# Hybrid HGRN and chunk-MLP backbone on one core: layer 1's modulation computed in two output phases instead of the HGRN stage

## The chip, the cores and the metric

The kernel runs on one core of a Trainium2 chip. The metric is device time in microseconds (us) of one execution; smaller is better. Engines: PE (TensorE) multiplies matrices into PSUM, PEld is its weight load, DVE (VectorE) and ACT (ScalarE) work elementwise, POOL (GpSimd) does small odds and ends, SP (SyncE) issues all the large DMA loads from one queue. Three runs of the kernel before took 2491.83, 2493.34 and 2493.70 us: the median is 2493.34 us. The execution that the profiler recorded took 2490.62 us, with a span of 2488.9 us from first to last instruction.

## The reference

Two layers over a 512-token latent stream `x` of width 1024 and, in layer 0, a 256-token context. Each layer is a half-step SwiGLU, a token mixer (layer 0: bidirectional HGRN2 with 8 heads; layer 1: a chunked spatial-gating MLP), and another half-step SwiGLU. Every sub-layer is modulated by vectors that come from the conditioning vector `c`:

```
def modulation(cond, w_mod, b_mod):
    m = jax.nn.silu(cond) @ w_mod + b_mod          # 9 vectors of 1024 per layer
def modulate(x, m, k):
    return x * (1 + m[..., 3*k+1, :]) + m[..., 3*k, :]
def post_norm_update(x, y, m, k, g, b):
    return layer_norm(DN_ALPHA * x + m[..., 3*k+2, :] * y, g, b)
```

So a layer needs nine modulation vectors, called channels here: 0, 1 and 2 (shift, scale, gate) for the first half-FFN, 3 to 5 for the mixer, 6 to 8 for the second half-FFN. Each is the product of one 1024-vector with a 1024 x 1024 matrix of its own (4 MB).

## The kernel before

Nearly all matrix products are done with float32 operands split into a high and a low part (`split`, L134: ACT copies the high part, DVE subtracts for the low one) and three matmuls per product (`mm3`, L146). A 128 x 1024 block of weights is loaded into one of three `raw` buffers and split into one of six `w` buffers (`unit`, L139).

The stages follow each other: layer 0's first half-FFN for latent and context, the HGRN mixer, layer 0's second half-FFN, layer 1's first half-FFN, the chunk MLP, layer 1's second half-FFN. A half-FFN has an input phase (`FeedIn` or `FeedSums`) and an output phase (`OutPhase`). `FeedSums.rest` (L577) goes over the hidden blocks f; a block loads its gate weights into `raw` and its up weights into `rawu` (two buffers) and forms sums of them in a tile `e` (two buffers); these three belong to the pool `sp`. In a block PE accumulates several products into one bank `psc`, and ACT copies that bank out (`kept`, L621) before PE adds the next product to it. `OutPhase.run` (L370) goes twice (half `hf` of the output columns) over 11 weight units; a unit needs one `w` split and two splits `hs` of the hidden blocks, and 24 matmuls. After the last unit come normalisation, transposes and the next stage's operand, which needs the channels of the next sub-layer (`operand_cols`, L226).

A modulation channel is a Python generator (`mod_task`, L172) of eight steps: a step loads 512 KB of the matrix (`mraw`, two buffers) and lets DVE multiply it with the row of silu(c) and sum, in two halves (`mod_dot`, L164, into a throwaway tile `junk` with the sums in `acc`; each half is a SCALAR_TENSOR_TENSOR and a DVE_READ_ACCUMULATOR). After the eighth step a few small instructions finish the channel; gates also need a PE transpose and a store. `mod_step(n)` (L203) adds n steps of credit and issues what the credit allows, behind a given instruction; `made(key)` (L216) issues whatever is still missing. The row of silu(c) comes from `silu_row` (L157): a load that broadcasts 4 KB to all 128 partitions and one ACT activation.

Instructions are written in program order with these hints; a scheduler then sets the order on each engine, and each engine runs its list in that order. DMA loads wait in SP's list for the buffer that they write.

In the HGRN stage (L912 to L1220) a loop of nine rounds runs over eight heads: round h projects head h (`proj_forget`, `proj_silu`) while the scores, states, outputs and gating of the heads before are worked off. `on` (L1149) is DVE's normalised output of a head, `pto` (L1155) its PE transpose, `Sc` (L1119) the scaled states that the output matmuls `po` (L1137 to L1139) read, `pkc` (L1094) the first matmul of a head's states. Four channels of layer 1 (1, 0, 4, 3) are queued in round 0 (L1197) and worked off at seven steps a round (L1205); `late_outputs` (L918) closes their pool in round 6 and opens the space for the last four heads' outputs. The remaining channels 5, 7, 6, 8 of layer 1 are computed in the chunk MLP (L1294, two steps per block, L1338).

Of the kernel before, what the change touches and what calls it, by code (L numbers as in the profile page):

```python
# [10 lines left out]
F32 = mybir.dt.float32  # L11
F32R = mybir.dt.float32r
# [6 lines left out]
P = 128  # L19
D = 1024  # L20
# [50 lines left out]
def backbone_kernel(  # L71
# [100 lines left out]
    def mod_task(modp, srow, l, ch, conds):  # L172
        accs = {c: modp.tile([P, KD, 2], F32, tag=f"acc_{c}", name=f"acc_{c}", bufs=2) for c in conds}
        for f in range(KD):
            raw = modp.tile([P, D], F32, tag="mraw", name="mraw", bufs=2)
            nc.sync.dma_start(raw, mod_w[l, ch, f])
            for c in conds:
                mod_dot(modp, accs[c][:, f, :], raw, srow[c])
            yield
        for c in conds:  # L180
            key = (l, ch, c)
            dot = modp.tile([P, KD], F32, tag="dot", name="dot", bufs=2)
            nc.vector.reduce_sum(dot, accs[c], axis=AX.X)
            if ch % 3 == 2:
                nc.vector.tensor_tensor(dot, dot, mbT[:, l, ch, :], ALU.add)
                pg = bank("pg")
                nc.tensor.transpose(pg[:KD, :P], dot, ident)
                row = modp.tile([KD, P], F32, tag="mrow", name="mrow", bufs=1)
                nc.vector.tensor_copy(row, pg[:KD, :P])
                gate_row[key] = dram.tile([1, D], F32, name=f"gr_{l}_{ch}_{c}")  # L190
                nc.sync.dma_start(gate_row[key].rearrange("o (f p) -> (o f) p", p=P), row)
            else:
                mod_col[key] = const.tile([P, KD], F32, name=f"mc_{l}_{ch}_{c}")
                nc.vector.scalar_tensor_tensor(
                    mod_col[key], dot, float(ch % 3), mbT[:, l, ch, :], ALU.add, ALU.add
                )

    def queue_mod(modp, srow, l, ch, conds):
        mod_queue.append(mod_task(modp, srow, l, ch, conds))
# [711 lines left out]

    with sbuf(name="hgo", bufs=1) as hgo, ExitStack() as late:  # L912
        hts = [hgo.tile([P, 2, T], F32R, name=f"ht{h}") for h in range(NH - NLATE)]
        early = ExitStack()
        modp = early.enter_context(sbuf(name="modp1", bufs=1, side="right"))
        srow = {"x": silu_row(modp, "x")}

        def late_outputs():  # L918
            for ch in (1, 0, 4, 3):
                made((1, ch, "x"))  # L920
            early.close()
            hgo2 = late.enter_context(sbuf(name="hgo2", bufs=1, side="right"))
            hts.extend(hgo2.tile([P, 2, T], F32R, name=f"ht{h}") for h in range(NH - NLATE, NH))

        with sbuf(name="hg", bufs=1) as hg:
            mask = []
# [237 lines left out]
            )  # L1164
            prev, done, last = None, None, None
            for h in range(NH + 1):
                if h == NH - NLATE + 2:
                    late_outputs()
                if h < NH:
                    n0, last = proj_forget(h, 0)  # L1170
                else:
                    op.lead(0, 1)
                if done and (h < NH or 0 == 0):
                    with tc.issue_after(last.ins):
                        gated(*done)
                if prev:
                    r0, r1 = prev
                    kTc = transposed([r.kk[:, NT + s, :] for r in prev for s in range(NTC)])
                    kT0 = transposed([r0.kk[:, s, :] for s in lat_order(0)[:-1]])
                    near_scores(r0)  # L1180
                    far_scores(0, r0)
                if h == NH and 0 == 1:
                    gated(*done)
                if h < NH:
                    n1, _ = proj_forget(h, 1)
                if prev:
                    context_states(h - 1, prev, kTc)
                    kT1 = transposed([r1.kk[:, s, :] for s in lat_order(1)[:-1]])
                    latent_states(h - 1, 0, r0, kT0)
                    far_scores(1, r1)  # L1190
                    latent_states(h - 1, 1, r1, kT1)
                if h < NH:
                    q, _ = proj_silu(h, 0, "q")
                    for r in (n0, n1):
                        ready = queries(r, q)
                    if h == 0:
                        for ch in (1, 0, 4, 3):  # L1197
                            queue_mod(modp, srow, 1, ch, ["x"])
                        first = ready
                else:  # L1200
                    if 0 == 2:
                        gated(*done)
                    op.lead(0, 2)
                if h < NH:
                    mod_step(7, first)  # L1205
                if prev:
                    on = outputs(h - 1, prev)
                    g, last = proj_silu(h - 1, 3, "g")
                    done = (h - 1, on, g)
                if h < NH:  # L1210
                    prev = (n0, n1)
# [11 lines left out]
    with sbuf(name="sp2", bufs=1) as sp, sbuf(name="hp2", bufs=1) as hp, bpools() as bp:  # L1223
        hget = f2.rest(hp, sp)
        xm = new_xm(xmp, "xm", T)
        f3 = FeedSums(
            1, 0, xm, NT,
            lambda i: hp.tile([P, T], F32, tag="h", name="h", bufs=NF).rearrange("p (k t) -> p k t", k=2),
        )
        op = OutPhase(  # L1230
            hget, NF, ffn_units(0, 1), NT, 0, 2, "x", 0.5, lambda t: x2[t], True, (1, 0),
            xm, lambda t: x3[t], f3, tail=3,
        )
        op.nhs, op.affine = 8, (0, 1)
        op.run(bp)
        hget = f3.rest(hp, sp)
        xm = new_xm(xmp, "xm", T)

        gin = GateIn(xm, lambda i: hp.tile([P, T], F32, tag="h", name="h", bufs=NF).rearrange("p (k t) -> p k t", k=2))
        op = OutPhase(  # L1240
            hget, NF, ffn_units(1, 0), NT, 1, 0, "x", 0.5, lambda t: x3[t], True, (1, 1),
            xm, lambda t: x4[t], gin, tail=3,
        )
        op.nhs, op.affine = 8, (0, 2)
        op.run(bp)


    with ExitStack() as vhp_stack:
# [9 lines left out]
        with sbuf(name="cm", bufs=1) as cm, ExitStack() as late:  # L1258
# [32 lines left out]
                stat.append((mv[:, 0:1], rstd))  # L1291
            modp = early.enter_context(swap("modp3"))
            srow = {"x": silu_row(modp, "x")}
            for ch in (5, 7, 6, 8):  # L1294
                queue_mod(modp, srow, 1, ch, ["x"])
            cu = late.enter_context(sbuf(name="cu", bufs=1))

# [5 lines left out]
            for gi in range(NG):  # L1303
                vt = vs[gi]
                for t in range(NT):
                    mean, rstd = stat[t]
                    nc.vector.tensor_scalar(vt[:, t, :], vt[:, t, :], mean, rstd, ALU.subtract, ALU.mult)
                ht = vhp.tile([P, 3, T], F32, tag="vh", name="ht")
                if gi == NG - 1:
                    for ch in (5, 7, 6, 8):  # L1310
                        made((1, ch, "x"))
                    early.close()
                for ci in range(3):
                    w = unit(cm_wu[gi * 3 + ci])
                    psu = bank("pscu")
                    feat_mm(psu, w, xm, 0, T)
                    u = cu.tile([P, T], F32, tag="u", name="u", bufs=2)
                    nc.scalar.activation(u, psu, AF.Gelu_apprx_tanh)
                    if gi == NG - 1 and ci == 2:
                        op.lead(0, 2)  # L1320
                    pss = bank("pscs")
                    for t in range(NT):
                        nc.tensor.matmul(
                            pss[:, t * P : (t + 1) * P], vt[:, t, ci * P : (ci + 1) * P], wsT[:, gi, :],
                            start=True, stop=True,
                        )

                    j = gi * 3 + ci
                    add = cu.tile([P, 1, P], F32, tag="add", name="add", bufs=2)
                    nc.vector.scalar_tensor_tensor(  # L1330
                        add[:, 0, :], wsum[:, gi, :], gb[:, 1, j : j + 1], bsr[:, gi, :], ALU.mult, ALU.add
                    )
                    tb = cu.tile([P, NT, P], F32, tag="tb", name="tb", bufs=2)
                    nc.vector.scalar_tensor_tensor(
                        tb, pss.rearrange("p (n t) -> p n t", t=P), gb[:, 0, j : j + 1],
                        add.broadcast_to([P, NT, P]), ALU.mult, ALU.add,
                    )
                    mod_step(2)  # L1338
                    nc.vector.tensor_tensor(ht[:, ci, :], tb.rearrange("p n t -> p (n t)"), u, ALU.mult)
                hs.append(ht)  # L1340
# [91 lines left out]
```

## Time and profile before

| | before |
|---|---|
| three runs, median (lowest to highest) | 2493.34 us (2491.83 to 2493.70) |
| profiled execution: time, span | 2490.62 us, 2488.9 us |
| PE, PEld busy | 2430.3 us (98%), 2185.5 us (88%) |
| DVE, ACT busy | 1919.8 us (77%), 1133.7 us (46%) |
| mean DMA traffic | 147 GB/s |

A page of the profile gives busy time per engine, a picture of the span in 40 slices, the chain of waits that ends last, and groups of instructions with the idle time of their engine ahead of them. Windows count busy time of every engine in a stretch; a timeline lists instructions by start. A matmul's end is modelled and matmuls overlap, so PE's busy share says little about small gaps; how far apart the same instruction of two rounds starts says more.

### The profile page before, as it was taken

What the parts mean: (1) busy time and instruction counts of PE and PEld (TensorE: products, weight loads), DVE (VectorE), ACT (ScalarE), POOL (GpSimd) and SP (SyncE); (2) the same over time, 40 slices, a digit from 0 to 9 for tenths busy, and PEclk for the clock granted to TensorE, in tenths of its full rate; (3) what the DMA queues carried; (4) which work ended last, traced back from release to release, by engine and by line L of the source; (5) the groups of instructions that cost most, each with busy time, mean ns of one, the idle gap of its engine ahead of it and who ended that gap; (6) DMA issues with size and microseconds to landing.
All of it is one profiled execution on the core that took longest, in us unless ns stands there. A gap on an engine that the chain in (4) does not pass through costs nothing.

```text
span 2488.9 us, 37370 instructions
## 1 busy us (share of the span) xinstructions
PE 2430.3 (98%) x14619; PEld 2185.5 (88%) x14619; DVE 1919.8 (77%) x3426; ACT 1133.7 (46%) x1725; POOL 46.5 (2%) x83
## 2 busy tenths in 40 slices
PE   7999999999988999999999999999999999999998
PEld 5888889988877888899988999988988888999986
DVE  7965678685699986998765988757889665998765
ACT  4222434453444543555643555534552233555641
POOL 0000000000000000000000000000000000000001
PEclk9999999999999999999999999999999999999999
DMA  8855556874345223333334333333347343332332
GB/s 319 299 196 199 177 183 198 286 257 140 102 137 160 77 60 117 133 132 107 119 103 134 103 110 111 111 95 123 119 160 260 129 148 106 140 128 102 102 110 73
DMA packets 106706, 364.92 MB, mean 147 GB/s; under 512 B 12392, under 2 KB 13600, under 8 KB 106528
## 3 DMA queue, kind: packets, MB, share of 16 engines
q1 hardware_dynamic: 106528, 362.53, 43.9%
q8 instruction: 114, 1.87, 0.3%
q14 instruction: 64, 0.52, 0.1%
HBM read 349.87 MB, written 12.61 MB: 146 GB/s over the span
## 4 chain that ended last, share of the span: by engine, by line
PE 80%; DVE 13%; DMA 2%; ACT 2%; issue 1%; POOL 1%; SPq 0%; POOLq 0%; DVEq 0%; ACTq 0%
PE y L150 8%; PE y L148 8%; PE y L149 8%; PE psf L149 5%; PE psf L150 5%; PE psf L148 5%; PE psc L148 5%; PE psc L150 5%; PE psc L149 5%; PE pse L148 2%; PE pse L150 2%; PE pse L149 2%; PE pscu L148 2%; PE pscu L149 2%; PE pscu L150 2%; DVE junk L170 1%
## 5 line engine op out<-in xcount | busy, mean ns | idle before, releaser
L136 DVE TENSOR_TENSOR w<-raw,w 128x1024 fp32r<-128x1024 f32 (+2 forms) x446 | 505.9, 1138 | 153.9 <-ACT w L135 153.0
L135 ACT ACTIVATE w<-raw 128x1024 fp32r<-128x1024 f32 (+2 forms) x446 | 439.5, 987 | 332.1 <-PE y L150 89.0
L150 PE MATMUL y<-w,hs 128*128 128x512 f32 x984 | 383.1, 389 | 1.0 <-DVE hs L136 1.0
L148 PE MATMUL y<-w,hs 128*128 128x512 f32 x984 | 383.3, 389 | 0.0
L149 PE MATMUL y<-w,hs 128*128 128x512 f32 x984 | 382.9, 389 | 0.0
L136 DVE TENSOR_TENSOR hs<-h,hs 128x512 fp32r<-128x512 f32 (+1 forms) x220 | 136.4, 637 | 143.6 <-ACT hs L135 143.4
L135 ACT ACTIVATE hs<-h 128x512 fp32r<-128x512 f32 (+1 forms) x220 | 127.3, 588 | 251.7 <-PE y L150 241.7
L150 PEld LDWEIGHTS y<-w,hs 128*128 128x128 f32 x984 | 184.7, 188 | 40.4 <-DVE hs L136 1.9
L148 PEld LDWEIGHTS y<-w,hs 128*128 128x128 f32 x984 | 184.7, 188 | 38.6 <-ACT hs L135 0.2
L149 PEld LDWEIGHTS y<-w,hs 128*128 128x128 f32 x984 | 184.7, 188 | 38.0
L148 PE MATMUL psf<-xm,w 128*128 128x512 f32 (+1 forms) x544 | 192.8, 361 | 17.8 <-ACT xm L135 17.1
L149 PE MATMUL psf<-xm,w 128*128 128x512 f32 (+1 forms) x544 | 194.4, 358 | 0.7 <-DVE xm L136 0.5
L150 PE MATMUL psf<-xm,w 128*128 128x512 f32 (+1 forms) x544 | 193.9, 357 | 0.8 <-DVE w L136 0.8
L170 DVE SCALAR_TENSOR_TENSOR junk<-mraw,srow_x 128x512 bf16<-128x512 f32 x256 | 167.3, 688 | 8.9 <-DMA mraw<-in_mod_w 8.8
L148 PE MATMUL pse<-f,w 128*128 128x256 f32 x480 | 136.1, 284 | 3.7 <-ACT w L135 3.7
L148 PE MATMUL psc<-f,w 128*128 128x256 f32 x480 | 136.1, 284 | 0.0
L150 PE MATMUL pse<-f,w 128*128 128x256 f32 x480 | 135.9, 283 | 0.0
L148 PE MATMUL psc<-xm,w 128*128 128x256 f32 x480 | 135.8, 283 | 0.0
L149 PE MATMUL psc<-xm,w 128*128 128x256 f32 x480 | 135.8, 283 | 0.0
L149 PE MATMUL pse<-f,w 128*128 128x256 f32 x480 | 135.8, 283 | 0.0
L150 PE MATMUL psc<-xm,w 128*128 128x256 f32 x480 | 135.8, 283 | 0.0
L149 PE MATMUL psc<-f,w 128*128 128x256 f32 x480 | 135.8, 283 | 0.0
(305 smaller groups left out, 5987.1 us busy)
## 6 DMA issues: line engine op xcount, KB each, us to landing
raw<-in_ffn_w_in SPq DMA_DIRECT2D x160, 512.0 KB, 4.3
mraw<-in_mod_w SPq DMA_DIRECT2D x144, 512.0 KB, 4.3
raw<-in_ffn_w_out SPq DMA_DIRECT2D x110, 512.0 KB, 3.6
rawu<-in_ffn_w_in SPq DMA_DIRECT2D x60, 512.0 KB, 3.5
x<-x SPq DMA_DIRECT2D x36, 512.0 KB, 3.4
raw<-in_hg_wf SPq DMA_DIRECT2D x32, 512.0 KB, 3.8
raw<-in_cm_wu SPq DMA_DIRECT2D x24, 512.0 KB, 4.6
raw<-in_cm_w_out SPq DMA_DIRECT2D x24, 512.0 KB, 3.5
```

What stands on the lines that cost most here:

```text
L135: nc.scalar.activation(dst_hi, src, AF.Copy)
L136: latest[0] = nc.vector.tensor_tensor(dst_lo, src, dst_hi.bitcast(F32), ALU.subtract)
L148: nc.tensor.matmul(ps, ah, bh, start=start, stop=False, **kw)
L149: nc.tensor.matmul(ps, ah, bl, start=False, stop=False, **kw)
L150: return nc.tensor.matmul(ps, al, bh, start=False, stop=stop, **kw)
L170: nc.vector.scalar_tensor_tensor(junk, w[:, c], 1.0, s[:, c], ALU.mult, ALU.mult, dst[:, i : i + 1])
```

## The change

Channels 1, 0, 4 and 3 of layer 1 leave the HGRN stage, with their pool, their row of silu(c) and `late_outputs`; the space for the last four heads' outputs is now taken at the stage's start. Channel 5 leaves the chunk MLP. Channels 1 and 0 are queued for the output phase of layer 0's second half-FFN at one step per weight unit, and channels 4, 3 and 5 for the output phase of layer 1's first half-FFN at one and a half. They use idle tiles of the input phases: the matrix loads go to the two `rawu` buffers, the row of silu(c) to one `e` buffer, and all small tiles (`acc`, `junk`, `dot`, `mrow`) are cut from the other `e` buffer. The throwaway `junk` is now float32 and one buffer instead of bfloat16 and two.

```diff
+    class Scraps:
+        def __init__(self, pool, small, ring):
+            self.pool, self.ring, self.at, self.got = pool, ring, 0, {}
+            self.small = pool.tile([P, D], F32, tag=small, name=small, bufs=2)
+        def tile(self, shape, dtype, tag, name, bufs=1):
+            if tag == "mraw":
+                return self.pool.tile(shape, dtype, tag=self.ring, name=self.ring, bufs=2)
...
+            t = self.small[: shape[0], a : a + int(np.prod(shape[1:]))]
...
+    def scraps(sp, l, chs):
+        s = sp.tile([P, D], F32, tag="e", name="e", bufs=2)
+        nc.sync.dma_start(s, cond[CI_OF["x"]].partition_broadcast(P))
+        nc.scalar.activation(s, s, AF.Silu)
+        small = Scraps(sp, "e", "rawu")
+        for ch in chs:
+            queue_mod(small, {"x": s}, l, ch, ["x"])
...
-        early = ExitStack()
-        modp = early.enter_context(sbuf(name="modp1", bufs=1, side="right"))
-        srow = {"x": silu_row(modp, "x")}
-        def late_outputs():
...
+        hgo2 = late.enter_context(swap("hgo2"))
+        hts.extend(hgo2.tile([P, 2, T], F32R, name=f"ht{h}") for h in range(NH - NLATE, NH))
...
-                if h == NH - NLATE + 2:
-                    late_outputs()
...
-                    if h == 0:
-                        for ch in (1, 0, 4, 3):
-                            queue_mod(modp, srow, 1, ch, ["x"])
-                        first = ready
...
-                if h < NH:
-                    mod_step(7, first)
...
         op.nhs, op.affine = 8, (0, 1)
-        op.run(bp)
+        scraps(sp, 1, (1, 0))
+        op.run(bp, None, 1)
...
         op.nhs, op.affine = 8, (0, 2)
-        op.run(bp)
+        scraps(sp, 1, (4, 3, 5))
+        op.run(bp, None, 1.5)
...
-            for ch in (5, 7, 6, 8):
+            for ch in (7, 6, 8):
                 queue_mod(modp, srow, 1, ch, ["x"])
```

DVE in the HGRN stage, from the sum `ssum` of a head's scores to the gated output `ht`. `junk,acc_x<-mraw,srow_x` is half a modulation step. Before:

```order
L1133 TENSOR_TENSOR ssum<-sT_5512,sT_5513 128x512
L988 TENSOR_TENSOR g<-psq,g 128x512
L1018 TENSOR_SCALAR X<-psfl 128x512
L170 SCALAR_TENSOR_TENSOR junk,acc_x<-mraw,srow_x 128x512 x2
L136 TENSOR_TENSOR w<-raw,w 128x1024
L170 SCALAR_TENSOR_TENSOR junk,acc_x<-mraw,srow_x 128x512 x2
L1144 TENSOR_REDUCE ss<-on 128x4
L1019 TENSOR_SCALAR X<-psfc 128x256
L1145 TENSOR_SCALAR ss<-ss 128x4
L136 TENSOR_TENSOR w<-raw,w 128x1024
L170 SCALAR_TENSOR_TENSOR junk,acc_x<-mraw,srow_x 128x512 x2
L1149 TENSOR_TENSOR on_6390<-po,rs 128x512
```

Six halves stand between the two splits and the reduction that lead to `on`; with the change no such row is left in this stage.

ACT near the end of layer 0's second input phase. `e<-e` is the activation silu(c) in the `e` buffer; `sc<-psc` are the copies of the bank that PE goes on accumulating into. With the change:

```order
L651 ACTIVATE sc<-psc 128x256
L135 ACTIVATE w<-rawu 128x1024
L135 ACTIVATE w<-raw 128x512
L222 ACTIVATE e<-e 128x1024
L651 ACTIVATE sc<-psc 128x256
L667 ACTIVATE silu<-silu 128x256
L135 ACTIVATE w<-raw 128x1024
L670 ACTIVATE silu<-psc 128x256
L135 ACTIVATE w<-e 128x1024
```

Before, the same list has no `e<-e` row: `sc<-psc` follows `w<-raw 128x512` at once. One `w<-e` comes after it and then none, so the activation stands two blocks ahead of the phase's end. The second input phase has the same picture.

SP at the same place, with the change (`raw<-in_ffn_w_out` are the output phase's weight units, `rawu<-in_mod_w` the modulation's loads, `e<-in_cond` the row of c):

```order
L628 DMA raw<-in_ffn_w_in 128x1024
L630 DMA rawu<-in_ffn_w_in 128x1024
L141 DMA raw<-in_ffn_w_out 128x1024
L221 DMA e<-in_cond 128x1024
L176 DMA rawu<-in_mod_w 128x1024
L141 DMA raw<-in_ffn_w_out 128x1024
L176 DMA rawu<-in_mod_w 128x1024
L141 DMA raw<-in_ffn_w_out 128x1024 x5
L176 DMA rawu<-in_mod_w 128x1024 x3
L141 DMA raw<-in_ffn_w_out 128x1024
```

Before, loads of the next input phase's `rawu` stand where the first two modulation loads stand now, and the weight units follow without anything between them.

## Rows read from the trace of the kernel before

**Rows 1.** The page: span, busy time, the chain of waits by engine, and the group of the output phases' matmuls that has any idle time of PE ahead of it (busy us, mean ns, idle us).

```profile
span 2488.9 us, 37370 instructions
...
PE 2430.3 (98%) x14619; PEld 2185.5 (88%) x14619; DVE 1919.8 (77%) x3426; ACT 1133.7 (46%) x1725; POOL 46.5 (2%) x83
...
PE 80%; DVE 13%; DMA 2%; ACT 2%; issue 1%; POOL 1%; SPq 0%; POOLq 0%; DVEq 0%; ACTq 0%
...
L150 PE MATMUL y<-w,hs 128*128 128x512 f32 x984 | 383.1, 389 | 1.0 <-DVE hs L136 1.0
```

**Rows 2.** Busy time of all engines in six windows of the HGRN stage, each from one head's first `pkc` to the next head's (stretch, its length, then PE, PEld, DVE, ACT, POOL busy with their instruction counts, granted clock, DMA share, GB/s).

```profile
681.10:729.40 48.30, 40.06 (x229) 35.14 (x228) 46.02 (x127) 21.61 (x33) 1.92 (x1) 0.93 0.44 141
729.40:773.10 43.70, 38.91 (x228) 34.33 (x227) 42.24 (x112) 19.41 (x29) 1.02 (x1) 0.96 0.46 146
773.10:813.20 40.10, 37.32 (x229) 32.90 (x228) 38.10 (x97) 19.08 (x29) 1.31 (x1) 1.00 0.46 143
813.20:852.20 39.00, 37.33 (x229) 32.90 (x228) 36.41 (x89) 18.62 (x29) 1.01 (x1) 1.00 0.29 95
852.20:889.60 37.40, 37.02 (x227) 32.77 (x227) 31.34 (x72) 18.71 (x31) 1.01 (x1) 1.00 0.20 57
889.60:927.00 37.40, 37.04 (x228) 32.77 (x227) 31.33 (x72) 18.68 (x30) 1.01 (x1) 1.00 0.19 57
```

**Rows 3.** The modulation's DVE work alone (tile `junk`) in the first four of these windows.

```profile
681.10:729.40 48.30, 14.07 (x43) 0.93 0.44 141
729.40:773.10 43.70, 12.17 (x38) 0.96 0.46 146
773.10:813.20 40.10, 8.02 (x23) 1.00 0.46 143
813.20:852.20 39.00, 2.86 (x10) 1.00 0.29 95
```

**Rows 4.** Who PE waited for: first from 641 to 852 us, then (last row) from 852 to 1000 us.

```profile
PE pto L1155 <- DVE on L1149: 10.1, 3, 5.3
PE po L1138 <- DVE Sc L1119: 4.1, 2, 2.3
PE po L1137 <- DVE Sc L1119: 3.1, 3, 1.5
...
PE po L1138 <- DVE Sc L1119: 1.1, 3, 0.4
```

**Rows 5.** Timeline of DVE and PE around the longest of these waits (start, duration, instruction).

```profile
714.90 0.69 DVE L1149 TENSOR_TENSOR on<-po,rs 128x512 f32<-128x512 f32 x1
...
715.65 1.12 PE L1155 MATMUL pto<-ident,on 128*128 128x128 f32 x4 [5.27 <-DVE on L1149]
```

**Rows 6.** The two stretches at a granted clock of 0.50 in these heads (columns as in rows 2).

```profile
713.70:720.50 6.80, 4.85 (x23) 4.86 (x24) 5.51 (x13) 4.40 (x6) 0.94 (x1) 0.50 0.86 298
761.50:764.90 3.40, 3.40 (x18) 3.40 (x17) 3.36 (x5) 2.16 (x4) 0.00 (x0) 0.50 0.55 170
```

**Rows 7.** Windows of output phases: layer 0's first half-FFN, all engines and then the tile `junk` alone; then layer 0's second and layer 1's first half-FFN, all engines.

```profile
260.00:380.00 120.00, 120.00 (x532) 99.27 (x532) 87.98 (x162) 46.42 (x62) 1.59 (x4) 1.00 0.54 177
...
260.00:380.00 120.00, 23.60 (x72) 1.00 0.54 177
...
1241.00:1350.00 109.00, 109.00 (x483) 90.24 (x482) 62.81 (x79) 45.37 (x63) 0.00 (x0) 1.00 0.34 108
1595.00:1705.00 110.00, 110.00 (x487) 91.11 (x486) 62.44 (x80) 44.67 (x62) 0.37 (x2) 1.00 0.33 100
```

**Rows 8.** DVE in an output phase: the `hs` splits of two weight units that follow each other.

```profile
1311.38 1.37 DVE L136 TENSOR_TENSOR hs<-h,hs 128x512 fp32r<-128x512 f32 x2 [1.61 <-ACT hs L135]
...
1316.83 1.37 DVE L136 TENSOR_TENSOR hs<-h,hs 128x512 fp32r<-128x512 f32 x2 [2.58 <-ACT hs L135]
```

**Rows 9.** DMA issues (count, KB each, median us from issue to landing).

```profile
mraw<-in_mod_w SPq DMA_DIRECT2D x144, 512.0 KB, 4.3
raw<-in_ffn_w_out SPq DMA_DIRECT2D x110, 512.0 KB, 3.6
...
srow_x<-in_cond SPq DMA_DIRECT2D x3, 512.0 KB, 5.9
```

**Rows 10.** ACT at the activation of the row of c at the HGRN stage's start.

```profile
577.99 1.06 ACT L161 ACTIVATE srow_x<-srow_x 128x1024 f32<-128x1024 f32 x1 [4.21 <-DMA srow_x<-in_cond]
```

**Rows 11.** Timelines of SP, DVE, ACT and PE near the end of layer 0's second input phase.

```profile
1208.20 0.33 SPq L141 DMA_DIRECT2D raw<-in_ffn_w_out  x1
1217.36 0.33 SPq L601 DMA_DIRECT2D rawu<-in_ffn_w_in  x1
...
1212.94 0.69 DVE L568 SCALAR_TENSOR_TENSOR raw<-raw,e 128x512 f32<-128x512 f32 x1
...
1216.17 0.63 ACT L135 ACTIVATE w<-raw 128x512 fp32r<-128x512 f32 x1
1217.61 0.39 ACT L622 ACTIVATE sc<-psc 128x256 f32<-128x256 f32 x1 [0.81 <-PE psc L150]
...
1218.85 0.28 PE L148 MATMUL psc<-xm,w 128*128 128x256 f32 x1
```

**Rows 12.** PE's waits for DVE in the context's output phase (510 to 575 us), then in the chunk MLP (1840 to 2008 us), and the tile `junk` in the chunk MLP.

```profile
PE y L150 <- DVE hs L136: 1.0, 2, 0.6
...
PE pscs L1323 <- DVE vt L1307: 1.7, 1, 1.7
...
1842.00:1950.00 108.00, 42.42 (x128) 1.00 0.74 246
```

More of the change, by code (lines that the diff above doesn't have):

```diff
@@ L196, in mod_task @@
                 )
+    class Scraps:
[5 more added lines that the diff above has]
+                return self.pool.tile(shape, dtype, tag=self.ring, name=self.ring, bufs=2)
+            got = self.got.setdefault(tag, [0])
+            if got[0] < bufs and tag != "junk" or len(got) == 1:
+                got.append(self.at)
+                self.at += int(np.prod(shape[1:]))
+                assert self.at <= D
+            a = got[1 + got[0] % (len(got) - 1)]
+            got[0] += 1
+            t = self.small[: shape[0], a : a + int(np.prod(shape[1:]))]
+            return t.rearrange("p (k i) -> p k i", i=shape[2]) if len(shape) > 2 else t
+    def scraps(sp, l, chs):
[5 more added lines that the diff above has]
+            queue_mod(small, {"x": s}, l, ch, ["x"])
     def queue_mod(modp, srow, l, ch, conds):
@@ L913, in backbone_kernel @@
         hts = [hgo.tile([P, 2, T], F32R, name=f"ht{h}") for h in range(NH - NLATE)]
-        early = ExitStack()
-        modp = early.enter_context(sbuf(name="modp1", bufs=1, side="right"))
-        srow = {"x": silu_row(modp, "x")}
-        def late_outputs():
-            for ch in (1, 0, 4, 3):
[L920 to L923, printed above, removed]
+        hgo2 = late.enter_context(swap("hgo2"))
+        hts.extend(hgo2.tile([P, 2, T], F32R, name=f"ht{h}") for h in range(NH - NLATE, NH))
         with sbuf(name="hg", bufs=1) as hg:
@@ L1172, in backbone_kernel @@
                     op.lead(0, 1)
-                if done and (h < NH or 0 == 0):
+                if done:
                     with tc.issue_after(last.ins):
@@ L1181, in backbone_kernel @@
                     far_scores(0, r0)
-                if h == NH and 0 == 1:
-                    gated(*done)
                 if h < NH:
@@ L1194, in backbone_kernel @@
                     for r in (n0, n1):
-                        ready = queries(r, q)
-                    if h == 0:
-                        for ch in (1, 0, 4, 3):
-                            queue_mod(modp, srow, 1, ch, ["x"])
-                        first = ready
-                else:
-                    if 0 == 2:
-                        gated(*done)
+                        queries(r, q)
+                else:
                     op.lead(0, 2)
-                if h < NH:
-                    mod_step(7, first)
                 if prev:
@@ L1309, in backbone_kernel @@
                 if gi == NG - 1:
-                    for ch in (5, 7, 6, 8):
+                    for ch in (7, 6, 8):
                         made((1, ch, "x"))
```

## The prediction

> **What bounds the kernel now.** I read the page first. PE is busy 98% of the span and carries 80% of the chain of waits; DVE carries 13% [rows 1]. That leaves 58.6 us in which PE is idle (2488.9 less 2430.3), so a change that only moves DVE work can win at most a part of that, plus what a lowered clock costs. The next question is where DVE ends last. PE's waits answer it: between 641 and 852 us PE waits 10.1 us for `on`, and 4.1 and 3.1 us for `Sc`, all of them DVE results [rows 4]. Behind that, the same kinds of wait are down to about a microsecond.
>
> The best view is a table of equal work. From one head's first `pkc` to the next, PE runs the same round, 227 to 229 matmuls. These rounds take 48.3, 43.7, 40.1 and 39.0 us and then settle at 37.4 us twice [rows 2]. In the slow ones DVE is busy 36.4 to 46.0 us, in the settled ones 31.3 us. The modulation's work in the same windows is 14.07, 12.17, 8.02 and 2.86 us [rows 3], and none in the settled ones, whose DVE work fits under 37.4. The timeline shows how it bites: `on` starts at 714.90, and PE, idle for 5.27 us, begins its transposes at 715.65 [rows 5]; in DVE's list six half steps stand between `ssum` and `on`. [...]
>
> **What is removed: the HGRN stage.** The four moved channels are 32 steps, 64 halves. Without them the DVE list of every round is that of the settled rounds, and PE's list too. So the four slow rounds should take 37.4 us each: 48.3 + 43.7 + 40.1 + 39.0 = 171.1 less 4 x 37.4 = 149.6 gives 21.5 us. That takes in the two stretches at half clock, which cost 0.5 x 10.2 = 5.1 us of it. The bounds: 19 us, if the first round still needs some 2.5 us to fill, as nothing excludes; and 23.0 us if also the settled rounds' own 0.4 us of PE idle (37.40 less 37.02) went in four rounds. I take 21.5, since the settled rows are the same work in the same order.
>
> The removed row of c and the emptied `late_outputs` gate nothing: ACT idles 4.21 us for that row at 577.99 [rows 10], but no wait of PE follows from it in rows 4. I cost their going at 0; the table load that now stands closer to ACT's first copies could take back its 1.3 us at most.
>
> **What is added: 40 steps in two output phases.** The pitch of a weight unit there is 5.45 us (1316.83 less 1311.38) [rows 8]. DVE is busy 62.81 of 109.00 and 62.44 of 110.00 us, PE all of it [rows 7]. A step costs DVE 23.60 us / 18 = 1.31 us (72 rows are 18 steps) [rows 7]. Sixteen steps add 21 us to the first phase and bring DVE to 84 of 109; 24 add 31 and bring it to 94 of 110. So DVE stays under PE in both, and the work lies beside matmuls. The first output phase runs such a mix already, 18 steps with DVE at 87.98 of 120.00, and PE is busy 120.00 [rows 7]. In all 984 matmuls of that row PE idles 1.0 us [rows 1], and that is the context's phase, whose units are half as long [rows 12]. Cost: 0; the other bound, from the context's 1.0 us for nine steps, scaled to 40, is 4.4 us, less a gain that I see no room for.
>
> The DMA follows: a step's load lands in 4.3 us, a unit's in 3.6 [rows 9]. With two `rawu` buffers a step can come every (4.3 + 1.3) / 2 = 2.8 us; 5.45 / 1.5 = 3.6 us are asked. The chunk MLP takes 246 GB/s on the way without PE waiting for weights [rows 12].
>
> **What is added: a load and a silu in each input phase's end.** This is the term that costs. The row of c goes into the `e` buffer that was last read by L568 at 1212.94 + 0.69 = 1213.63 us [rows 11]. SP, which issued the weight unit ahead of it at 1208.20, holds the load until then; the load behind it was free only at 1217.36 anyway, so SP's list loses nothing. A broadcast of this row takes 5.9 us to land [rows 9]: 1219.5. ACT comes to it early: the activation stands behind the split that starts at 1216.17 and ends at 1216.80, so ACT idles from there, as it did 4.21 us for the same load [rows 10]. The activation takes 1.06 us: 1220.6. Behind it stands the copy of `psc` that now starts at 1217.61; it would end at 1220.6 + 0.39 = 1221.0. PE may not go on accumulating into that bank before, and wants to at 1218.85 [rows 11]: 2.2 us of waiting. Nothing else in the block is late by as much. The second input phase has the same list, so 2 x 2.2 = 4.4 us. Bounds: 0, if the load lands in 3.6 us like a weight unit (1217.2, and the copy ends at 1218.7); and 2 x (2.2 + 3.4) = 11.2, if each wait were followed by 6.8 us at half clock like the first of rows 6. I take 4.4, because the 5.9 us are of the very same load.
>
> [...]
>
> **The chunk MLP** loses eight steps of 32. DVE had room there; its one PE wait, 1.7 us for `vt` [rows 12], has the same DVE list ahead of it as before. Cost and gain 0, between 0 and 1.7 us gained.
>
> **Sum.** 21.5 - 4.4 = 17.1 us. Against the profiled execution's own 2490.6 us: 2473.5. The median of the runs is 2.7 us above that execution, so the forecast for the median is 2493.3 - 17.1 = 2476.2, written as 2476.
>
> **Rivals.**
> A: the silu's load hides. For it: SP has nothing else in flight then. Against: three loads of this row have a median of 5.9 us, whatever was beside them. Time: 2493.3 - 21.5 = 2472.
> B: each new PE wait is followed by a stretch at half clock. For it: rows 6. Against: the wait that ends the third slow round comes with a clock of 1.00 over the whole window, with 2.8 us of idle PE [rows 2]. With 3.4 us at 0.50, the shorter row, each costs 1.7 us: 2476.2 + 3.4 = 2479.6; with the longer one 2483.
> [...]
> C, on the other side: the slow rounds are not slow through the modulation. For it: the fourth is 1.6 us over 37.4 with only 2.86 us of it, and these rounds also have twice the DMA share (0.44 against 0.20). Against: what lengthens them falls with the modulation's share, and the loads go too. Then only the silu's price is left: 2493.3 + 4.4 = 2498.
> D, also slower: in the output phases the weight units stand on SP behind loads that wait for DVE, and DVE's splits behind steps that wait for loads. Once the six `w` buffers are drained, a unit would take 4.3 + 1.3 + 3.6 + about 2.2 for its two splits = 11.4 us instead of 5.45. Three such units eat the gain; eight, where the list of the second phase has two loads between units, would give 2493.3 - 17.1 + 48 = 2524. Against: the first output phase has the same mix, and six units ahead are 33 us.
> E: the change does not do what it says, since the channels come so late that the phases' ends wait for them. At one step per unit, 16 steps are done by unit 17 of 22, and 24 at one and a half by the same unit, five units or 27 us ahead of the end. Were they two units late, it would cost 11 us in each: 2498.
>
> **How the numbers follow.** Forecast 0.60, A 0.18, B 0.11, C 0.03, D 0.04, E 0.04. A measurement can tell 0.2%, 5 us, from no change: faster means below 2488.4. Forecast, A and B lie there whole, and some of E's smaller lateness: 0.91; within 0.2%: 0.05, from small forms of D and E; slower: 0.04. The forecast's own bounds are 19 to 23 us gained in the heads and up to 4.4 lost in the output phases; with A and B they give 2470 to 2484.
>
> **What would show it.** In the changed profile the rounds from `pkc` to `pkc` are 37 to 38 us from the second head on, DVE about 31 us in each, with no half clock there. ACT waits some 2.7 us for `e<-in_cond` in each of two input phases, and PE about 2 us for `sc` right after. The output phases show no PE wait for `hs` or `w`. I am wrong if the early rounds stay above 39 us, if PE waits in the output phases, or if the copies of `psc` are on time.

## The result, and the profile after

The changed kernel takes 2472.35 us (median of 4 runs, 2471.74 to 2473.67), the kernel before, run beside it, 2492.59 us (4 runs, 2490.63 to 2493.7). The ratio is 0.9919 with a 95% interval of 0.9907 to 0.9931: 20.2 us less. The forecast was 2476 us, 17 us less, with a range of 2470 to 2484.

The page of the changed kernel, its span, its busy times and the chain of waits by engine:

```profile
span 2470.9 us, 37394 instructions
...
PE 2426.5 (98%) x14619; PEld 2181.9 (88%) x14619; DVE 1919.2 (78%) x3426; ACT 1133.4 (46%) x1726; POOL 45.5 (2%) x83
...
PE 83%; DVE 11%; ACT 2%; issue 2%; DMA 1%; POOL 1%; SPq 0%; POOLq 0%; DVEq 0%; ACTq 0%
```

Beside [rows 1], DVE does the same work as before to within a microsecond (1919.2 against 1919.8 us). What fell is PE's idle time, from 58.6 to 44.4 us, and DVE's share of the chain. This is a change of place, not of amount.

The rounds of the HGRN stage, cut at each head's first `pkc` like [rows 2] and with the same columns:

```profile
682.50:719.90 37.40, 37.11 (x228) 32.84 (x227) 31.26 (x72) 18.47 (x30) 1.02 (x1) 1.00 0.17 57
719.90:757.40 37.50, 37.14 (x229) 32.87 (x228) 31.32 (x72) 18.79 (x31) 1.02 (x1) 1.00 0.18 57
757.40:794.80 37.40, 37.05 (x228) 32.79 (x228) 31.32 (x72) 18.70 (x31) 1.01 (x1) 1.00 0.19 57
794.80:832.20 37.40, 37.04 (x228) 32.77 (x227) 31.33 (x72) 18.69 (x31) 1.01 (x1) 1.00 0.19 57
832.20:869.70 37.50, 37.13 (x229) 32.86 (x228) 31.34 (x72) 18.78 (x31) 1.01 (x1) 1.00 0.19 57
869.70:907.10 37.40, 37.04 (x228) 32.77 (x227) 31.32 (x72) 18.70 (x31) 1.01 (x1) 1.00 0.18 57
```

All six are settled rounds now, with 72 DVE instructions in 31.3 us and the clock at 1.00. The first four take 149.7 us where they took 171.1: 21.4 us gained. PE's waits from 641 to 852 us, beside [rows 4]:

```profile
PE po L1159 <- DVE Sc L1140: 1.7, 5, 0.4
PE pssn L1094 <- DVE B L1076: 0.5, 1, 0.5
```

The wait for `on` (10.1 us) is gone, and so are both stretches at half clock of [rows 6]. The two output phases that took the work, beside the last two lines of [rows 7]:

```profile
1221.00:1330.00 109.00, 109.00 (x483) 90.25 (x482) 81.58 (x150) 46.05 (x63) 0.00 (x0) 1.00 0.56 186
1575.00:1685.00 110.00, 110.00 (x488) 90.97 (x487) 91.28 (x186) 45.47 (x63) 0.00 (x0) 1.00 0.65 206
```

DVE went from 62.8 and 62.4 us to 81.6 and 91.3, and PE is busy all of both stretches. Then ACT at the new silu, in the first and in the second input phase, and the landing of the row (count, KB, median us):

```profile
1196.68 0.63 ACT L135 ACTIVATE w<-raw 128x512 fp32r<-128x512 f32 x1
1197.61 1.06 ACT L222 ACTIVATE e<-e 128x1024 f32<-128x1024 f32 x1 [0.29 <-DMA e<-in_cond]
1198.58 0.36 ACT L651 ACTIVATE sc<-psc 128x256 f32<-128x256 f32 x1
...
1550.62 0.63 ACT L135 ACTIVATE w<-raw 128x512 fp32r<-128x512 f32 x1
1551.97 1.06 ACT L222 ACTIVATE e<-e 128x1024 f32<-128x1024 f32 x1 [0.72 <-DMA e<-in_cond]
...
e<-in_cond SPq DMA_DIRECT2D x2, 512.0 KB, 3.7
```

ACT waits 0.29 and 0.72 us for the row, not 2.7. The copy of `psc` ends at 1198.58 + 0.36 = 1198.94, and this PE row shows that it is in time, with 0.42 us to spare and no idle time noted:

```profile
1199.36 0.28 PE L148 MATMUL psc<-xm,w 128*128 128x256 f32 x1
```

Between the two profiled executions the span fell by 18.0 us, less than the heads gave. 1.5 us of the difference were lost before the heads, and they are no mark of the change. The first `psv` product (count, ns min/median/max, first and last start) in the kernel before, the changed one, and one of the experiments below (each half done twice) whose code is the changed kernel's up to there:

```profile
L148 PE MATMUL psv<-w,xm x64: 389/389/476, 571.8 to 627.5; 128*128 128x512 f32 x64
L148 PE MATMUL psv<-w,xm x64: 389/389/476, 573.3 to 628.9; 128*128 128x512 f32 x64
L148 PE MATMUL psv<-w,xm x64: 388/389/476, 572.4 to 628.0; 128*128 128x512 f32 x64
```

The same code starts it at 572.4 and at 573.3. With the experiments below that leave this part alone, the old code up to there starts it between 571.8 and 573.1 us in five kernels, the new code between 571.7 and 573.3 in four. Of the other 1.9 us, lost behind the heads, 1.5 went in one stretch at half clock that the last section shows: ahead of it the changed execution leads by 19.2 us, behind it by 17.7. The medians over the runs are the better measure of the total.

### The profile page after: what moved, and what is told of

Same layout as the page of the kernel before. It is cut to its first block, busy times and chain, and to the rows that moved or that the text cites. A ratio compares the mean times of both kernels' runs of the same rounds, so it can differ in the third digit from the quotient of the medians.

```text
span 2470.9 us, 37394 instructions
## 1 busy us (share of the span) xinstructions
PE 2426.5 (98%) x14619; PEld 2181.9 (88%) x14619; DVE 1919.2 (78%) x3426; ACT 1133.4 (46%) x1726; POOL 45.5 (2%) x83
## 4 chain that ended last, share of the span: by engine, by line
PE 83%; DVE 11%; ACT 2%; issue 2%; DMA 1%; POOL 1%; SPq 0%; POOLq 0%; DVEq 0%; ACTq 0%
PE y L150 8%; PE y L149 8%; PE y L148 8%; PE psf L149 6%; PE psf L150 6%; PE psf L148 6%; PE psc L148 5%; PE psc L150 5%; PE psc L149 5%; PE pse L148 2%; PE pse L150 2%; PE pse L149 2%; PE pscu L148 2%; PE pscu L149 2%; PE pscu L150 2%
## 5 line engine op out<-in xcount | busy, mean ns | idle before, releaser
L148 PE MATMUL psc<-f,w 128*128 128x256 f32 x480 | 136.1, 284 | 0.0
L149 PE MATMUL psc<-f,w 128*128 128x256 f32 x480 | 135.8, 283 | 0.0
L150 PE MATMUL psc<-f,w 128*128 128x256 f32 x480 | 135.8, 283 | 0.0
```

The source lines that it names most:

```text
L148: nc.tensor.matmul(ps, ah, bh, start=start, stop=False, **kw)
L149: nc.tensor.matmul(ps, ah, bl, start=False, stop=False, **kw)
L150: return nc.tensor.matmul(ps, al, bh, start=False, stop=stop, **kw)
```

## Experiments

**Products or loads?** The prediction put the slow heads down to DVE's products, rival C to the loads. One kernel keeps every load and shortens the products, the other keeps the products and drops the loads. Both start from the kernel before.

```diff
+    short = []
...
-            c = slice(i * n, (i + 1) * n)
+            c = slice(i * n, i * n + (8 if pool in short else n))
...
         modp = early.enter_context(sbuf(name="modp1", bufs=1, side="right"))
+        short.append(modp)
```

> The kernel before, all its loads of modulation weights kept in the HGRN stage, but each of the 64 halves there sums 8 columns in place of 512 (so layer 1's channels 1, 0, 4 and 3 are sums over 16 of 1024 columns; the rest is unchanged). Theory, that DVE's products made the heads slow: the four slow rounds fall from 48.3, 43.7, 40.1 and 39.0 us to 37.4 to 38.5 each, and the time to about 2472 to 2475 us. Rival C, that the loads' share of the DMA made them slow: the rounds stay at 39 to 48 us, the time at 2488 to 2493 us.

```diff
+            if modp in dry:
+                raw = srow["x"]
+            else:
+                raw = modp.tile([P, D], F32, tag="mraw", name="mraw", bufs=2)
+                nc.sync.dma_start(raw, mod_w[l, ch, f])
...
         modp = early.enter_context(sbuf(name="modp1", bufs=1, side="right"))
+        dry.append(modp)
```

> The mirror image: the kernel before without the 32 weight loads of the HGRN stage; the 64 halves stay at full length, but multiply the row of c with itself in place of a weight row (so layer 1's channels 1, 0, 4 and 3 are not computed). Theory (DVE's products): the rounds stay within a microsecond of 48.3, 43.7, 40.1 and 39.0 us and the time at 2488 to 2493 us; if anything the halves come sooner, because none waits for a load, and the first rounds hold more of them. Rival C (the loads): 37.4 us a round and 2471 to 2474 us.

Measured: with short products 2477.87 us (0.9945 of before, 0.9922 to 0.9968), without loads 2491.57 us (0.9999, 0.9988 to 1.001). The rounds, first of the kernel with short products, then of the one without loads:

```profile
682.10:721.50 39.40, 37.37 (x229) 32.81 (x228) 31.58 (x115) 18.68 (x29) 1.02 (x1) 1.00 0.62 201
721.50:761.80 40.30, 37.35 (x229) 32.90 (x228) 34.80 (x127) 18.97 (x30) 1.02 (x1) 1.00 0.61 197
761.80:800.90 39.10, 37.35 (x229) 32.90 (x228) 33.82 (x97) 20.16 (x32) 1.01 (x1) 1.00 0.33 107
```

```profile
681.70:734.40 52.70, 42.44 (x228) 37.20 (x227) 49.90 (x140) 21.32 (x34) 1.77 (x1) 0.87 0.04 11
734.40:774.20 39.80, 37.35 (x229) 32.97 (x228) 38.80 (x101) 19.31 (x29) 1.46 (x1) 1.00 0.17 54
774.20:814.30 40.10, 37.41 (x228) 32.81 (x227) 39.13 (x98) 20.36 (x30) 1.31 (x1) 1.00 0.25 79
814.30:853.10 38.80, 37.30 (x228) 32.91 (x227) 33.72 (x78) 18.57 (x29) 1.01 (x1) 1.00 0.25 82
```

Without loads the DMA share of the first round is 0.04, and the four rounds take 52.7 + 39.8 + 40.1 + 38.8 = 171.4 us, as before (171.1); more halves fall into the first round, as none waits for a load. The products alone are enough for the whole loss, and rival C falls. But the theory's numbers for the short products were missed: three rounds are still 1.7 to 2.9 us over 37.4, 6.6 us in all, and 2477.87 lies above the 2475 expected. What DVE and PE waited for in that kernel, from 641 to 810 us, and DVE's wait in the kernel before in the same stretch:

```profile
DVE junk L172 <- DMA mraw<-in_mod_w: 11.7, 8, 3.7
...
PE pkl L1118 <- ACT kT L1066: 4.5, 3, 2.4
PE po L1141 <- DVE Sc L1122: 2.2, 3, 1.1
```

```profile
DVE junk L170 <- DMA mraw<-in_mod_w: 3.2, 6, 1.6
```

DVE stands 11.7 us at steps whose load has not landed, and what stands behind such a step in its list is late: the longest wait, 3.7 us, ends at 713.24, and behind it the second `X` of that round (L1022) starts 5.95 us after the first (713.42 less 707.47), where a settled round has 2.78 (858.53 less 855.75). PE's two waits, 6.7 us, match the 6.6 us lost. In the kernel before, DVE's wait for loads is 3.2 us; that its long products cover the landings is likely, but no run tests it. The weights' loads did not hold PE up: none of its waits in the kernel with short products, from 641 to 810 us, is for a `w`. So the loads do not slow the heads by their share of the DMA (0.62 and 0.61 in its first two rounds, which are 2.0 and 2.9 us over, against 0.44 and 0.46 before, which were 10.9 and 6.3 over), but a step whose load is late costs DVE's time just like a product. Moving steps and loads together removed both.

**How much can a round of the heads hold?** DVE is busy 31.3 of 37.4 us, so 6.1 us are free on paper. One kernel spreads the 32 steps of before thinner, and each head's behind that head's own queries (`ready`) where all stood behind the first head's (`first`); one leaves a single channel of the changed kernel in the heads, with the pool, the row of c and `late_outputs` that it needs there (not in the diff below).

```diff
                 if h < NH:
-                    mod_step(7, first)
+                    mod_step(5, ready)
```

> The kernel before with the same modulation in the HGRN stage, spread thinner: 5 steps a head in place of 7, queued behind the head's own queries. DVE has 37.4 - 31.3 = 6.1 us free in a settled round; 10 halves take 10 x 0.68 = 6.8 us. Theory, that the sum of DVE's work in a round decides: rounds of 38.1 us, five or six of them, so 6 x 0.7 = 4 us lost of the 21.5, and about 2475 us. Rival, that the place decides (any half that stands ahead of `on` delays PE, as in the third slow round, which had about as many halves and took 40.1 us): five rounds near 40 us, 5 x 2.7 = 13.5 us lost, and about 2484 us.

```diff
+                    if h == 0:
+                        queue_mod(modp, srow, 1, 1, ["x"])
...
+                if h < NH:
+                    mod_step(2, ready)
...
-        scraps(sp, 1, (1, 0))
+        scraps(sp, 1, (0,))
```

> The changed kernel, but with one of the moved channels (layer 1's channel 1) still in the HGRN stage, two steps in each of four rounds; the first output phase then has eight steps in place of sixteen. Four halves with their read-outs are 4 x 0.76 = 3.0 us a round, half of the 6.1 us that DVE has free in a settled round. Theory, that the place decides: in a settled round of the changed kernel DVE's only holes are 1.71 us ahead of `ss`, 1.19 ahead of `on` and 2.09 ahead of `X`, and all else stands without a gap; the four halves stand in one lump ahead of `on`, where 1.7 us are free, so `on` is some 1.3 us late and the four rounds take up to 38.7 us, about 2475 to 2477 us. Rival, that the sum of a round decides: 31.3 + 3.0 = 34.3 us is under 37.4, nothing is lost, 2472 us.

Measured: 2486.61 us (0.9979 of before, 0.9967 to 0.999) and 2472.05 us (0.9913, 0.9897 to 0.993). The rounds with 5 steps a head, then those with 2:

```profile
682.00:723.60 41.60, 37.58 (x229) 32.95 (x228) 40.98 (x109) 21.04 (x33) 1.02 (x1) 1.00 0.38 124
723.60:762.10 38.50, 37.46 (x228) 32.84 (x227) 37.46 (x95) 17.69 (x27) 1.02 (x1) 1.00 0.42 129
...
840.30:879.60 39.30, 37.44 (x228) 32.85 (x227) 34.71 (x89) 18.63 (x28) 1.01 (x1) 1.00 0.37 119
879.60:922.50 42.90, 38.76 (x229) 34.38 (x228) 37.41 (x89) 20.37 (x33) 1.01 (x1) 0.96 0.20 62
```

```profile
682.30:721.50 39.20, 37.34 (x229) 32.90 (x228) 35.05 (x84) 20.13 (x32) 1.02 (x1) 1.00 0.25 82
721.50:758.90 37.40, 37.04 (x228) 32.77 (x227) 33.70 (x80) 18.69 (x30) 1.02 (x1) 1.00 0.27 85
758.90:796.40 37.50, 37.06 (x228) 32.81 (x227) 34.03 (x84) 18.74 (x30) 1.01 (x1) 1.00 0.18 57
```

Five steps a round cost 1.1 to 1.9 us in each of the middle four rounds. The six rounds take 240.5 us against 6 x 37.4 = 224.4, 16.1 us over. The total is near the 13.5 of "the place decides" and far from the 4 of "the sum decides", but not in the way either had it: the middle rounds lose less than the 2.7 us of the one and more than the 0.7 of the other, and 9.7 us are lost in the first and the last round. PE's longest wait in that kernel, from 641 to 925 us, is no longer for `on`:

```profile
PE pkl L1115 <- ACT kT L1063: 7.2, 5, 4.1
```

Two steps a round, a lump of four halves ahead of `on`, cost nothing in a round that has settled; there "the place decides" missed (up to 38.7 us expected, 37.4 and 37.5 measured), and only the first round is 1.8 us longer. So neither rule holds alone. Of the 6.1 us, two steps' products of 2.5 us a round fit at no loss, and five steps' do not; where between them the loss begins was not tested. Where DVE's holes lie is seen in its list of a settled round of the changed kernel:

```profile
853.07 0.69 DVE L1165 TENSOR_REDUCE ss<-on 128x4 f32<-128x512 f32 x1 [1.71 <-ACT on L1163]
...
855.14 0.69 DVE L1170 TENSOR_TENSOR on<-po,rs 128x512 f32<-128x512 f32 x1 [1.19 <-POOL rs L1168]
...
858.53 0.42 DVE L1040 TENSOR_SCALAR X<-psfc 128x256 f32<-128x256 f32 x1 [2.09 <-PE psfc L150]
```

The holes of over a microsecond lie within some 7 us, around `on`. Elsewhere no hole reaches half a microsecond, and `Sc` and what `kT` is made from stand there. That what is added among them comes late for PE fits the wait of 7.2 us for `kT`; no run moved the steps alone.

**How much can an output phase hold?** In the changed kernel every half of the two phases is done twice.

```diff
             for c in conds:
-                mod_dot(modp, accs[c][:, f, :], raw, srow[c])
+                for _ in range(2 if isinstance(modp, Scraps) else 1):
+                    mod_dot(modp, accs[c][:, f, :], raw, srow[c])
```

> The changed kernel with every half of the two output phases done twice (the second writes the same sum again), so 64 and 96 halves where 32 and 48 are. DVE's busy time would go from 81.6 to 81.6 + 32 x 0.68 = 103.4 of 109 us in the first phase and from 91.3 to 91.3 + 48 x 0.68 = 123.9 of 110 us in the second. Theory, that DVE's sum is what hides or not: the first phase within 2 us of 109, the second about 14 us longer, together 2486 to 2490 us. Rival, that the cover was already spent and DVE's in-order list delays `hs` long before it is full: the first phase is longer too, by 5 to 22 us, and the time over 2495 us.

Measured: 2477.64 us (0.9938 of before, 0.9915 to 0.9961), 5.3 us more than the changed kernel, where the theory had 14. The second phase, its window and the one wait of PE at its end:

```profile
1575.50:1685.50 110.00, 110.00 (x490) 91.26 (x489) 109.83 (x254) 45.99 (x65) 0.00 (x0) 1.00 0.60 195
...
PE pg L188 <- DVE e L186: 6.5, 1, 6.5
```

DVE is busy 109.83 of 110.00 us and PE still does not wait for an `hs`. It waits at the end, 6.5 us for the gate made from the last channel. The estimate of 14 us put everything that DVE cannot do in the 110 us on PE's path. But `hs` is made ahead into eight buffers, so it is the modulation's own end that comes late. That is rival E's mechanism, and this is its price; 48 more halves of 0.68 us bring it on, so the changed kernel is some 33 - 6.5 = 26 us of DVE work away from it, an estimate from this one point that takes the wait to grow as the work does. In the first phase DVE went to 99.29 of 109.00 us, and PE did not wait at all.

**What does a late row of c cost?** The row is loaded through POOL's queue, with the same order on ACT, DVE and PE; and once in pieces of 64 bytes, where ACT takes the silu two instructions later.

```diff
-        nc.sync.dma_start(s, cond[CI_OF["x"]].partition_broadcast(P))
+        nc.gpsimd.dma_start(s, cond[CI_OF["x"]].partition_broadcast(P))
```

> The changed kernel with the two loads of the row of c issued by POOL in place of SP; the order on ACT, DVE and PE is the same, so only the landing moves. In the changed kernel the row landed 3.3 to 3.7 us after its issue, ACT started 0.3 and 0.7 us late, and the copy of `psc` was done some 0.4 us before PE wanted the bank. Theory, that the term was right in its mechanism and only its landing was too long: every microsecond of landing beyond 0.4 later than now is a microsecond of PE waiting for `sc`, in each of two phases: landing 2 us later costs 2 x 1.6 = 3.2 us, about 2476 us; no later, nothing. Rival, that PE does not depend on that copy at this place: no wait for `sc` at all however late the row lands, and 2472 us.

```diff
-        nc.sync.dma_start(s, cond[CI_OF["x"]].partition_broadcast(P))
+        for b in range(2): nc.sync.dma_start(*(v.rearrange("p (a b c) -> p b a c", b=2, c=16)[:, b] for v in (s, cond[CI_OF["x"]].partition_broadcast(P))))
```

> The changed kernel with each load of the row of c cut into two loads of 32 pieces of 64 bytes for every partition, so that it lands late; ACT then takes the silu two instructions later, behind the copy of `psc` and a product, ahead of a split and of the next copy. Theory: ACT stands at the silu until the row has landed, everything behind it (the split of a weight, the next copy of `psc`) is late by as much, and PE waits; with a landing of 10 to 20 us PE waits 6 to 16 us in each of two phases, 2485 to 2505 us. Rival, that ACT's list has enough slack there: the row lands late and PE waits less than 2 us, 2472 to 2476 us.

Measured: 2472.72 us (0.9926 of before, 0.9906 to 0.9946) and 2473.9 us (0.9931, 0.9911 to 0.995). ACT and PE with the load through POOL, in the first of the phases:

```profile
1195.50 0.63 ACT L135 ACTIVATE w<-raw 128x512 fp32r<-128x512 f32 x1
1197.66 1.06 ACT L222 ACTIVATE e<-e 128x1024 f32<-128x1024 f32 x1 [1.53 <-DMA e<-in_cond]
...
1199.04 0.39 PE L148 MATMUL psc<-xm,w 128*128 128x256 f32 x1 [0.70 <-ACT sc L651]
```

From the start of the split to the silu it is 2.16 us here and 0.93 in the changed kernel: the row is 1.23 us later. Less the 0.42 us to spare that is 0.81, and PE waits 0.70. In the second phase the row is 0.65 us later and PE's wait for `sc` is 0.5 us; there the changed kernel had almost nothing to spare, since its copy of `psc` ends at 1553.30 and PE's matmul starts at 1553.35. So the mechanism of the 4.4 us is real, and beyond the slack its price is close to one for one; the rival, that PE does not depend on the copy, falls. In small pieces the row let ACT stand 2.43 and 2.36 us at the silu, with PE waiting 0.9 and 1.0 us for `sc`. The landing of 10 to 20 us that was expected there, a guess of mine that no trace had shown, did not come: ACT starts the silu 7.1 us after the first load's issue (1199.36 less 1192.3). So that run tells little more.

**What is left.** One more channel leaves the context's output phase for layer 0's second one; then the chunk MLP's channels are queued later as well, by one group of chunks (the second diff) and by two (`gi == 2` there).

```diff
-        for l, ch in ((0, 5), (0, 7), (0, 6), (0, 8), (1, 2)):
+        for l, ch in ((0, 5), (0, 7), (0, 6), (0, 8)):
...
-        scraps(sp, 1, (1, 0))
-        op.run(bp, None, 1)
+        scraps(sp, 1, (1, 0, 2))
+        op.run(bp, None, 1.5)
```

> The changed kernel with one more channel (layer 1's channel 2) moved out of the context's output phase, into the second output phase of layer 0 (three channels there, one and a half steps a unit). The doubled products showed that DVE can be busy to the last tenth there before PE waits; this adds 8 x 1.31 = 10.5 us to 82 of 109 us. Theory: nothing is lost there, and the context's phase loses its last waits for `hs` (0.8 and 0.6 us): 1 to 2 us gained, about 2471 us. Rival, that a third channel comes too late for the gate of its own phase's end, as the fifth channel did with doubled products: PE waits for `e` at about 1330 us and the time is 2474 to 2480 us.

```diff
-            for ch in (7, 6, 8):
-                queue_mod(modp, srow, 1, ch, ["x"])
...
             for gi in range(NG):
                 vt = vs[gi]
+                if gi == 1:
+                    for ch in (7, 6, 8):
+                        queue_mod(modp, srow, 1, ch, ["x"])
```

> As the run before, and the last three channels of the chunk MLP are queued one group of chunks later, behind the first normalisations of `vt`, for which PE waits 1.8 us. Theory: the wait goes, and the time is about 1.5 us under the run before, 2469 us. Rival, that `vt` is late because of the normalisation's own chain (statistics, then the subtraction) and not through the modulation: no difference.

> The changed kernel with layer 1's channel 2 moved into layer 0's second output phase (as before) and the last three channels of the chunk MLP queued two groups of chunks later, so that no product stands among the first normalisations of `vt`. Theory: PE's wait of 1.8 us for `vt` goes, and some or all of the stretch at half clock near 2114 us with it: 2467 us. Rival, that `vt` waits for its own statistics: no difference to the run with the gate moved, 2469 us.

Measured: 2469.14 us (2468.09 to 2469.54), 2469.07 us (2468.22 to 2469.4) and 2468.55 us (2467.89 to 2468.75), 4 runs each; in ratios to before 0.9911 (0.9896 to 0.9926), 0.991 (0.9894 to 0.9927) and 0.99 (0.9885 to 0.9915). None of these 12 runs is as slow as the fastest of the changed kernel, 2471.74. PE's waits in the context's output phase of the changed kernel, and the first `psv` with the channel moved:

```profile
PE y L150 <- DVE hs L136: 0.8, 2, 0.6
PE y L148 <- ACT hs L135: 0.6, 1, 0.6
```

```profile
L148 PE MATMUL psv<-w,xm x64: 389/389/476, 570.3 to 625.8; 128*128 128x512 f32 x64
```

With the channel moved PE has no wait in that phase, and none for the gate `e` at the end of the phase that took it, which was the rival. `psv` starts at 570.3 us, and at 570.1 in both kernels with the later queue; the nine others lie between 571.7 and 573.3. The medians differ by 3.2 us from the changed kernel's; each against the kernel before run beside it, the gain is 22.4 us against 20.2, so 2.1 us more, and the two intervals overlap. So the phase's waits are gone, and a gain of 1 to 2 us as expected fits, but its size is not settled. The later queue gave nothing that can be told apart, where 1.5 to 2 us were expected. PE's wait for `vt` in the changed kernel, and with the channels two groups later:

```profile
PE pscs L1334 <- DVE vt L1318: 1.8, 1, 1.8
```

```profile
PE pscs L1334 <- DVE vt L1318: 1.2, 1, 1.2
```

Queued one group later, some products still stood among the first normalisations, and the wait was 1.9 us. Two groups later none does, and 1.2 us of wait remain: two thirds are not the modulation's, as the rival said. Nor does the stretch at half clock near 2114 us tell: it is missing in both kernels with the later queue, but also in kernels that queue as before.

## Why the prediction was right, and where it was off

The direction, the place and the range held: 2472.35 lies in 2470 to 2484. But the sum is 3.7 us off, and the range holds the result because it took rival A in. One of the prediction's own signs of being wrong also came, that "the copies of `psc` are on time".

- The heads: 21.5 us predicted, 21.4 measured, by the reading that the changed rounds are the settled rounds of [rows 2]. The cause also stands, with one thing added by the short products: DVE's waits for loads are part of what the steps cost.
- The 40 steps in the output phases at nothing: right. The sums of 84 and 94 us were 2 to 3 us above the measured 81.6 and 91.3, since a step added 1.17 and 1.20 us to DVE's busy time and not 1.31. The doubled halves show that the cover reaches to DVE at 109.83 of 110.00 us. Rivals D and E did not come; E's price appeared only with twice the products. The chunk MLP at nothing: PE's wait for `vt` is 1.8 us, where it was 1.7.
- The silu's row: this is the term that was off. The step was "I take 4.4, because the 5.9 us are of the very same load." The row landed in 3.7 us, and 4.4 became 0; rival A's time, 2472, is the measured one. That the copy of `psc` keeps its place behind a waiting silu, on which the 4.4 rested, no row of the kernel before had shown; the load through POOL shows it. ACT begins the silu at 1197.66 there and the copy behind it at 1198.62, though the bank was ready at about 1196.94 (an estimate: 1.44 us behind the split's start at 1195.50, as in [rows 11]). So the mechanism was right; only the landing was mis-sized (3.7 us through SP, 3.9 through POOL), and with 0.05 us to spare in the second phase the 0 was a near thing. I had written that those loads took 5.9 us "whatever was beside them". That was the mistake, and two windows tell it, the kernel before while the old row was under way and the changed one while the new row was:

```profile
572.00:578.00 6.00, 6.00 (x29) 4.95 (x28) 5.24 (x7) 1.07 (x2) 1.67 (x3) 1.00 0.82 234
```

```profile
1194.20:1197.90 3.70, 3.70 (x33) 3.70 (x32) 3.22 (x5) 2.26 (x4) 0.00 (x0) 1.00 0.37 142
```

- The DMA share is 0.82 there and 0.37 here: SP had issued three weight loads in the 6 us ahead of the old row, and two loads within 1.6 us behind it, but none for 5 us ahead of the new one and none while it was under way. Of the loads of a row of c whose landing the two traces show one by one, those of 5.2 to 6.8 us have shares of 0.82 to 0.91, the one of 3.7 us has 0.43. No run changed the company alone. The nearest row was not the one with the same tile but one with little beside it; the 3.6 us of [rows 9] came closer.
- Rival B (half clock behind the new waits) had no waits to follow; where the experiments made such waits, of 0.5 to 1.0 us, no stretch at half clock came behind them: behind the 0.70 us with the load through POOL, PE's matmuls start 0.12 us apart from 1199.26 to 1200.69, where the stretch at half clock of the last section has 0.21 to 0.22. Rival C fell with the kernel without loads.
- The sum: 2492.6 less the 21.4 us of the heads is 2471.2; the median is 1.2 us above it, about as much as runs of one kernel differ by.

## What to carry to other kernels

Read an engine's room from where its consumer waits, not from its busy share: the same kind of DVE work cost 21 us in a stage where PE waits for each result, and where 2.5 of 6.1 free us a round could be filled at no loss but five steps could not; it cost nothing in a stage whose results are made eight buffers ahead, up to a DVE busy 109.83 of 110.00 us, as long as the work itself is not due at the stage's end. Compare equal rounds of the same work to get such a term to a few tenths of a microsecond. For a load's landing, take the row with the same traffic beside it, not the row of the same tile (the row landed here in 3.7 us, that row said 5.9).

## What was not expected of the hardware

The same 512 KB broadcast lands in 3.7 us with little beside it and in 5.9 us with weight loads ahead of it and behind it. A product of 8 columns in place of 512 still takes a quarter of the time: 163 ns and 83 ns for its read-out, against 690 ns and 84 ns (medians in the heads). Cutting the row into 64-byte pieces made ACT start the silu only 3.6 us later, counted from the split ahead of it (1199.36 - 1194.81 against 0.93 us). And PE ran 110 us without a gap beside a DVE that was busy 109.83 us of them.

The clock also told a kernel's executions apart where its code and its waits are the same. Late in layer 1, behind one and the same wait of PE (1.8 us for `xm`, before `psf`), this stretch of the changed kernel's execution and the same stretch of the one before, 19.2 us later there, read:

```profile
2114.00:2117.40 3.40, 3.40 (x18) 3.40 (x18) 2.47 (x4) 1.53 (x3) 0.29 (x1) 0.50 0.41 152
```

```profile
2133.20:2136.60 3.40, 3.40 (x31) 3.40 (x30) 2.92 (x5) 1.54 (x4) 0.33 (x1) 1.00 0.41 151
```

18 matmuls against 31 in the same 3.4 us, at a granted clock of 0.50 in the one and 1.00 in the other, which is worth some 1.7 us (half of 3.4; the lead fell by 1.5). In the profiled executions of all twelve kernels this wait of 1.8 us was followed by it in four and not in eight, so a microsecond or two between two executions is no verdict on an edit.
